# Three stretches of an elementwise product and GELU: the short stretch moved from the end of the y loads to their front

## The chip, the cores and the metric

The kernel runs on one core of one Trainium2 chip. The metric is the device time of one execution in microseconds (us), taken as the median of several runs. The profile is one further execution, recorded by the hardware profiler; its times run from the start of the first recorded instruction.

## The reference

Two float32 arrays of 1024 x 4096 are multiplied element by element, and the tanh form of GELU is applied to the product:

```
z = x * y
out = 0.5 * z * (1 + tanh(sqrt(2 / pi) * (z + 0.044715 * z ** 3)))
```

Each array has 16.78 MB. Both are read once and one is written once, 50.33 MB in all.

## The kernel before

The kernel is written without a scheduler: every queue's order and every wait is laid down by hand. The flat array is cut into three stretches, PIECES, and each stretch is spread over the 128 partitions so that a partition's share is one contiguous row in memory. The stretches are 1280, 16384 and 15104 columns of float32 for each partition, that is rows of 5 KB, 64 KB and 59 KB. They are called here the small, the first large and the second large stretch. All of x has its place in the buffer `xs`; y has a smaller buffer `ys` of 20440 columns, whose parts are used again. The product is written over x in `xs`, GELU is applied there in place, and the stores read `xs`.

- **Loads of x.** `load_x(0)` (small, issued by SP) and `load_x(1)` (first large, issued by ACT) are moved by `_hoist` to the very front of the program, ahead of its opening barriers. `load_x(2)` (second large) is issued by SP later.
- **Loads of y.** `Y_LOADS` lists start column, end column and place in `ys` of each load of y, in order of issue; all go through SP. Before the change these are the first large stretch, the second large one, and the small one last. SP waits for the small x (`sem_x[0]`) before it issues the first of them. `Y_FREE[i]` is the number of finished multiplications that load i waits for because it writes over an older part of `ys`.
- **VectorE (DVE)**, line 98, multiplies in pieces whose widths `STEPS` gives: four of 4096, then seven of 2048 and one of 768, then one of 1280. It waits for the load of y in question at line 95.
- **ScalarE (ACT)**, line 106, applies GELU to each piece after its multiplication.
- **Stores**, line 115, are issued by SP in the order of `STORES`: first large, second large, small. SP executes in order, so each store stands behind all loads and behind every earlier store's wait. The first store also waits (line 114 and the line before it) for `sem_y[-2]`, the last load of y but one, so that it is queued when one load is still in front of it.
- **End.** SP waits for all stores but the last (line 117), clears the semaphores (line 120) and then waits for the last store (line 121).

SP's DMAs all go through one queue, which the profile calls q1; ACT's single load has a queue of its own, q10.

Of the kernel before, what the change touches and what calls it, by code (L numbers as in the profile page):

```python
# [1 line left out]

# [4 lines left out]


F32 = mybir.dt.float32
GELU = mybir.ActivationFunctionType.Gelu_apprx_tanh  # L10

PIECES = [(0, 1280), (1280, 17664), (17664, 32768)]

Y_LOADS = [(1280, 17664, 4056), (17664, 32768, 0), (0, 1280, 15104)]

Y_FREE = [0, 3, 4]

STEPS = [[4096] * 4, [2048] * 7 + [768], [1280]]  # L20
STORES = [(1280, 17664), (17664, 32768), (0, 1280)]
Y_BUF = 20440


def _hoist(nc, issued):

    here = nc.cur_bb.bb.instructions
    first = nc.main_func.blocks[0].instructions
    for ins in issued:
        del here[next(k for k, i in enumerate(here) if i is ins or i.name == ins.name)]  # L30
    engine = issued[0].engine
    at = next(
        k
        for k, i in enumerate(first)
        if i.engine == engine and type(i).__name__ == "InstDrain"
    )
    first[at:at] = issued


@with_exitstack  # L40
def kernel(
    ctx: ExitStack,
    tc: tile.TileContext,
    x: bass.AP,
    y: bass.AP,
    out: bass.AP,
):
    nc = tc.nc
    P = nc.NUM_PARTITIONS

    def columns(t, a, b):

        flat = t.flatten_outer_dims().rearrange("r c -> (r c)")
        pa, pb = next(q for q in PIECES if q[0] <= a and b <= q[1])
        return flat[P * pa : P * pb].rearrange("(p c) -> p c", p=P)[:, a - pa : b - pa]


    tc.close()
    tc.compile()  # L59

    xs = nc.alloc_sbuf_tensor("xs", [P, PIECES[-1][1]], F32).ap()
    ys = nc.alloc_sbuf_tensor("ys", [P, Y_BUF], F32).ap()
    sem_x = [nc.alloc_semaphore(f"sem_x{i}") for i in range(len(PIECES))]
    sem_y = [nc.alloc_semaphore(f"sem_y{i}") for i in range(len(Y_LOADS))]
    sem_mul = nc.alloc_semaphore("sem_mul")
    sem_act = nc.alloc_semaphore("sem_act")
    sem_o = [nc.alloc_semaphore(f"sem_o{i}") for i in range(len(STORES))]

    def load_x(i, engine=nc.sync):
        a, b = PIECES[i]  # L70
        return engine.dma_start(out=xs[:, a:b], in_=columns(x, a, b)).then_inc(sem_x[i], 16)

    def load_y(i):
        a, b, r = Y_LOADS[i]
        return nc.sync.dma_start(
            out=ys[:, r : r + b - a], in_=columns(y, a, b)
        ).then_inc(sem_y[i], 16)

    _hoist(nc, [load_x(0).ins])
    _hoist(nc, [load_x(1, nc.scalar).ins])  # L80
    nc.sync.wait_ge(sem_x[0], 16)
    load_y(0)
    load_x(2)
    for i in range(1, len(Y_LOADS)):
        if Y_FREE[i]:
            nc.sync.wait_ge(sem_mul, Y_FREE[i])
        load_y(i)

    n = 0
    done = {}  # L90
    for i, (a, b, r) in enumerate(Y_LOADS):
        for j, (xa, xb) in enumerate(PIECES):
            if xa <= a < xb:
                nc.vector.wait_ge(sem_x[j], 16)
        nc.vector.wait_ge(sem_y[i], 16)  # L95
        c = a
        for w in STEPS[i]:
            nc.vector.tensor_mul(  # L98
                out=xs[:, c : c + w],
                in0=xs[:, c : c + w],  # L100
                in1=ys[:, r + c - a : r + c - a + w],
            ).then_inc(sem_mul, 1)
            n += 1
            done[c + w] = n
            nc.scalar.wait_ge(sem_mul, n)
            nc.scalar.activation(  # L106
                out=xs[:, c : c + w], in_=xs[:, c : c + w], func=GELU
            ).then_inc(sem_act, 1)
            c += w

    for i, (a, b) in enumerate(STORES):
        if i == 0:
            nc.sync.wait_ge(sem_y[-2], 16)
        nc.sync.wait_ge(sem_act, done[b])
        nc.sync.dma_start(out=columns(out, a, b), in_=xs[:, a:b]).then_inc(sem_o[i], 16)
    for i in range(len(STORES) - 1):
        nc.sync.wait_ge(sem_o[i], 16)
    nums = sorted(s.num for s in [*sem_x, *sem_y, *sem_o[:-1], sem_mul, sem_act])
    assert nums == list(range(nums[0], nums[-1] + 1))
    nc.sync.sem_clear(range(nums[0], nums[-1] + 1))  # L120
    nc.sync.wait_ge(sem_o[-1], 16).then_inc(sem_o[-1], -16)


# [1 line left out]
_INS = ['x', 'y']  # L125
_OUTS = [((1024, 4096), 'float32')]


# [23 lines left out]
```

## Time and profile before

| what | value |
|---|---|
| median of 3 runs | 119.79 us (119.72 to 119.82) |
| span of the profiled execution | 118.5 us (118.52 in the trace) |
| own time of the profiled execution | not recorded beyond its span; 119.79 - 118.52 = 1.27 us is how far the runs' median lies above it |
| VectorE busy | 35.2 us (30%), 13 instructions |
| ScalarE busy | 31.0 us (26%), 14 instructions |
| DMA | 50.33 MB, mean 425 GB/s; q1 82.2% and q10 16.5% of 16 engines' span |
| DMAs | 3 loads of x, 3 loads of y, 3 stores |

A share of "16 engines' span" is the sum of the times that all packets of a queue took, divided by 16 times the span. A packet here is one row of one partition, so each of the nine DMAs has 128 data packets, 8 for each of the 16 DMA engines, and one 4-byte packet for each engine that raises the semaphore. "us to landing" counts from a DMA's issue to its semaphore's last increment, the time spent behind other DMAs included.

### The profile page before, as it was taken

The page shows a single profiled execution, that of the slowest core. Times are in us where ns is not written, and L with a number is a line of the kernel's source. Part 1 is how long each engine was busy: PE and PEld are TensorE (multiplying, and loading weights), DVE is VectorE, ACT ScalarE, POOL GpSimd, SP SyncE. Part 2 cuts the span into 40 slices and gives each one's busy share as a digit, 9 for nine tenths or more (in the row PEclk, how much of TensorE's full clock was granted, in tenths as well). Part 3 has the DMA queues.
Part 4 walks back from the last instruction along what each step waited for, and adds up shares of the span by engine and source line. Part 5 has one row for each costly group of instructions (what it writes and reads, how often), then busy time and mean ns, then how long its engine had stood idle before and what let it go on. Part 6 is the DMA issues. An engine that isn't in the chain of part 4 may idle for free.

```text
span 118.5 us, 82 instructions
## 1 busy us (share of the span) xinstructions
DVE 35.2 (30%) x13; ACT 31.0 (26%) x14; POOL 0.2 (0%) x4
## 2 busy tenths in 40 slices
DVE  0000000000000069999920000059999940000000
ACT  4000000000000000977975000006998990000000
POOL 0000000000000000000000000000000000000000
DMA  9888899889988897797797797798899887977975
GB/s 492 382 382 382 354 575 487 354 354 398 664 354 354 354 652 326 326 652 326 326 632 347 326 632 347 326 575 354 354 531 531 354 354 326 652 326 326 652 326 221
DMA packets 1296, 50.33 MB, mean 425 GB/s; under 512 B 144, under 2 KB 144, under 8 KB 528
## 3 DMA queue, kind: packets, MB, share of 16 engines
q1 hardware_dynamic: 1152, 41.94, 82.2%
q10 hardware_dynamic: 144, 8.39, 16.5%
HBM read 33.55 MB, written 16.78 MB: 425 GB/s over the span
## 4 chain that ended last, share of the span: by engine, by line
DMA 55%; DVE 24%; ACT 3%; issue 1%; DVEq 0%
DMA ys<-in_y_dram 43%; DVE xs L98 24%; DMA xs<-in_x_dram 11%; ACT xs L106 3%; DVEq L95 0%
## 5 line engine op out<-in xcount | busy, mean ns | idle before, releaser
L98 DVE TENSOR_TENSOR xs<-xs,ys 128x2048 f32<-128x2048 f32 (+3 forms) x13 | 35.2, 2777 | 60.9 <-DMA ys<-in_y_dram 60.9
L106 ACT ACTIVATE xs<-xs 128x2048 f32<-128x2048 f32 (+3 forms) x13 | 29.7, 2301 | 65.1 <-DVE xs L98 65.1
L106 ACT ACT_TABLE_LOAD x1 | 1.3, 1283 | 1.6 <-PEq L59 1.6
L136 POOL MEMSET const-bfloat16-1.0<- 128x1 bf16 x1 | 0.1, 103 | 0.0
L136 POOL MEMSET const-uint8-127<- 128x1 uint8 x1 | 0.1, 102 | 0.0
L136 POOL MEMSET const-float32-0.0<- 128x1 f32 x1 | 0.1, 100 | 0.2 <-issue 0.2
L136 POOL MEMSET const-float32-1.0<- 128x1 f32 x1 | 0.1, 99 | 0.0
## 6 DMA issues: line engine op xcount, KB each, us to landing
xs<-in_x_dram SPq DMA_DIRECT2D x1, 7552.0 KB, 46.5
ys<-in_y_dram SPq DMA_DIRECT2D x1, 7552.0 KB, 22.5
out_dram<-xs SPq DMA_DIRECT2D x1, 7552.0 KB, 20.4
xs<-in_x_dram SPq DMA_DIRECT2D x1, 640.0 KB, 13.6
ys<-in_y_dram SPq DMA_DIRECT2D x1, 640.0 KB, 19.7
out_dram<-xs SPq DMA_DIRECT2D x1, 640.0 KB, 20.8
xs<-in_x_dram ACTq DMA_DIRECT2D x1, 30.4
ys<-in_y_dram SPq DMA_DIRECT2D x1, 29.0
```

What stands on the lines that cost most here:

```text
L98: nc.vector.tensor_mul(out=xs[:, c : c + w], in0=xs[:, c : c + w], in1=ys[:, r + c - a : r + c - a + w],).then_inc(sem_mul, 1)
L106: nc.scalar.activation(out=xs[:, c : c + w], in_=xs[:, c : c + w], func=GELU).then_inc(sem_act, 1)
L136: nc = _bacc.Bacc("TRN2", target_bir_lowering=False, num_devices=1)
```

## The change

The small stretch of y becomes the first load of y, issued without a wait for the small x. The load of y's second large stretch is cut in two, rows of 11264 columns (44 KB) and of 3840 columns (15 KB). The widths of the multiplications follow: the small piece comes first, the second large stretch is five pieces of 2048 and one of 1024 for the first part, one of 2048 and one of 1792 for the second. The small stretch is stored second, between the two large ones. `sem_y[-2]`, for which the first store waits, is now the 44 KB load.

```diff
-Y_LOADS = [(1280, 17664, 4056), (17664, 32768, 0), (0, 1280, 15104)]
+Y_LOADS = [(0, 1280, 0), (1280, 17664, 4056), (17664, 28928, 0), (28928, 32768, 11264)]
 
-Y_FREE = [0, 3, 4]
+Y_FREE = [0, 0, 3, 4]
 
-STEPS = [[4096] * 4, [2048] * 7 + [768], [1280]]
-STORES = [(1280, 17664), (17664, 32768), (0, 1280)]
+STEPS = [[1280], [4096] * 4, [2048] * 5 + [1024], [2048, 1792]]
+STORES = [(1280, 17664), (0, 1280), (17664, 32768)]
 Y_BUF = 20440
...
     _hoist(nc, [load_x(0).ins])
     _hoist(nc, [load_x(1, nc.scalar).ins])
-    nc.sync.wait_ge(sem_x[0], 16)
     load_y(0)
+    load_y(1)
     load_x(2)
-    for i in range(1, len(Y_LOADS)):
+    for i in range(2, len(Y_LOADS)):
         if Y_FREE[i]:
             nc.sync.wait_ge(sem_mul, Y_FREE[i])
         load_y(i)
```

## The prediction

> **What bounds the kernel now.** I read the page's DMA part first, because VectorE and ScalarE are busy for only 30% and 26% of the span.
>
> ```profile
> DMA packets 1296, 50.33 MB, mean 425 GB/s; under 512 B 144, under 2 KB 144, under 8 KB 528
> ...
> q1 hardware_dynamic: 1152, 41.94, 82.2%
> q10 hardware_dynamic: 144, 8.39, 16.5%
> HBM read 33.55 MB, written 16.78 MB: 425 GB/s over the span
> ```
>
> The two queues' packets together take 82.2 + 16.5 = 98.7% of the time of 16 DMA engines. Of 118.5 us an engine is without a packet for only 1.3%, 1.5 us. Next, the waits of SP's queue and the chain in order of time:
>
> ```profile
> SPq L75 <- DVE xs L98: 45.4, 2, 41.4
> SPq L117 <- DMA out_dram<-xs: 18.9, 1, 18.9
> SPq L115 <- ACT xs L106: 18.7, 2, 17.9
> SPq L115 <- DMA ys<-in_y_dram: 14.5, 1, 14.5
> SPq L75 <- DMA xs<-in_x_dram: 12.0, 1, 12.0
> ```
>
> ```profile
> 0.00 13.55 DMA xs<-in_x_dram
> 13.55 0.02 issue
> 13.57 28.99 DMA ys<-in_y_dram
> ...
> 55.78 22.47 DMA ys<-in_y_dram
> ```
>
> and last the DMA issues with their times to landing:
>
> ```profile
> xs<-in_x_dram SPq DMA_DIRECT2D x1, 7552.0 KB, 46.5
> ys<-in_y_dram SPq DMA_DIRECT2D x1, 7552.0 KB, 22.5
> out_dram<-xs SPq DMA_DIRECT2D x1, 7552.0 KB, 20.4
> xs<-in_x_dram SPq DMA_DIRECT2D x1, 640.0 KB, 13.6
> ys<-in_y_dram SPq DMA_DIRECT2D x1, 640.0 KB, 19.7
> out_dram<-xs SPq DMA_DIRECT2D x1, 640.0 KB, 20.8
> ```
>
> The waits look large, and the chain puts 13.55 us on the small load of x. But a wait of the issuing engine costs time only if the DMA engines run dry behind it. Adding issue time (from the timeline: 0, 13.57, 13.96, 55.78, 60.12, 78.27, 96.55, 97.71) and time to landing gives the landings: small x 13.55, first large x about 30.5, first large y 42.56, second large x 60.41, second large y 78.25, small y 79.82, then the stores at 99.19, 116.98 and 118.49. From 42.56 on each follows the one before by its own size: 60416-byte rows after 17.85 us (7.73 MB, 433 GB/s), 5120-byte rows after 1.57 us, 65536-byte rows after 19.37 us. These are eight packets in a row on each engine: 2.230 us, 0.196 us, 2.42 us each. A straight line through the first two has 0.0368 us for 1000 bytes and 0.0079 us for each packet whatever its size. So the kernel is a single uninterrupted stream of packets, and its time is the sum of packets plus what lies at the two ends. The packet records of the trace say the same: the first packet starts at 1.01 us, the last ends at 118.12, and between them the engines stand without a packet for about 0.09 us each at 79 us, and little else.
>
> **Where the 1.5 us of idle time lie.** 1.01 us ahead of the first packet; 118.52 - 118.12 = 0.40 us after the last one; the 0.09 us at 79 us, where the small y has run out (79.0 on the first engine) before the first store, issued at 78.27, has its packets ready (first at 79.11, so 0.84 us after the issue). The change touches only the last of these directly.
>
> **The change, part by part.**
>
> *The wait for the small x goes, and the small y is issued at about 1.5 us* (SP's last opening barrier ends then, by the trace). SP's 12.0 us of waiting vanish, but its cover was ACT's load of the first large x: from 10.8 us, when the last packet of the small x ends, to 14 us q10 alone kept all 16 engines in packets of 2.42 us. Nothing is gained. Now the small y's eight packets per engine stand there alternately with q10's. They cost the 1.57 us that they no longer cost at 78.25. The first large y therefore lands 1.57 later, at 42.56 + 1.57 = 44.1, and the second large x at 62.0. If the wait's cover were missing, it would cost up to 13.57 - 10.8 = 2.8 us.
>
> *The multiplications of the small stretch* (1.48 us on VectorE, 1.25 on ScalarE) move from 94.6 us into the empty time before 44 us, as the small y should land at around 25 us (alternating with the five large packets of x that are left at 10.8). Free.
>
> *The second large y as 44 and 15 KB rows.* The loads wait for two and three multiplications of 4096, at a pitch of 17.43 / 4 = 4.36 us: issued at about 53 and 57 us, while the second large x runs until 62.0. The cover is 5 to 9 us where it was 60.41 - 55.78 = 4.6. If it were gone, each microsecond late would cost one. Packets: by the line above 45056 bytes take 1.666 us and 15360 bytes 0.573. Eight of each are 13.33 + 4.58 = 17.91, where one load took 17.85: **+0.06 us**, and 0.01 for one more semaphore packet. The landings are 75.3 and 79.9.
>
> [...]
>
> *The first store* is issued when the 44 KB load lands, at 75.3, with 4.6 us of packets ahead instead of 1.57. The 0.84 us from issue to packet are covered now, so the 0.09 us at 79 us goes: **between -0.09 and 0**, since the engine that ends last had no such gap (its small y ends at 79.38, after 79.11). I take -0.04.
>
> *The order of the stores.* Small one second: its wait on ScalarE was met long before. The last store waits for the final GELU. VectorE starts the second large stretch at 75.4 and takes 5 x 2.2 + 1.1, ending at 87.6; the 15 KB part lands at 79.9, so VectorE goes on to 91.8 and ScalarE to about 93.5. The store is needed when the small store runs out, at 79.9 + 19.4 + 1.6 = 100.8: 7 us of cover, where the one before had 98.5 - 96.55 = 2. Nothing is gained, for it was covered already. The bytes cost the same in either order.
>
> *The end.* The last packet is now 59 KB. From the last packet's end to the last landing I count 0.44 us for that store in the trace and 0.37 for the small one: **+0.07**. Engines ended within 0.16 us of each other after either store; without the pause at 79 us to line them up they may end up to 0.38 apart (the spread at 79 us), whence a bound of +0.2. The semaphores were cleared at 117.06, under the last store, and will be cleared under it again, at about 101.
>
> Sum against the profile's 118.52: +0.07 - 0.04 + 0.07 = +0.1, so 118.6; with the 1.27 us by which the median of 119.79 lies above the span, **119.9 us**. Known bounds: -0.09 to +0.35.
>
> **Rivals.** A difference under 0.2%, 0.24 us, is about what a measurement of this kernel can tell from none.
>
> *Slower: alternating small and large packets costs more than their bytes.* In the opening 17.43 MB (both x loads and the first large y) land at 42.56. At the stream's 433 GB/s they need 40.25; with 1.01 in front and 0.36 behind that makes 41.6, so 0.95 us are lost there, in the only stretch in which small packets run beside a second queue. If they are the price of 0.64 MB of small packets among large ones, a second 0.64 MB pays it again: 119.9 + 0.95 = 120.8. It decides from 0.24 us on, when each of the 128 packets takes 30 ns more than 196. Against it: the packet records have 196 ns for most small packets between 4 and 11 us (196 to 225 by the microsecond), and 282 on average from 1 to 2 us, where they run alone. So most of the loss belongs to the start, which stays. Price by that row: up to 8 x 0.029 = 0.23.
>
> *Faster: the queue that is kept full gains.* If with q1 empty from 10.8 to 13.6 us the engines had run below their rate, the small y would fill gaps, together with the 0.09 at 79 us. The most that could come back is idle time, 1.5 - 1.01 - 0.40 = 0.1 us, and the 0.45 us by which the two x loads' packets exceed their later durations: 119.79 - 0.55 = 119.25. Against it: the slow packets lie in the first microseconds, ahead of the small y.
>
> *The engines' work becomes the bound* is excluded: they would have to end 7 us later.
>
> **How the numbers follow.** Forecast (no difference to be measured, 119.9): 0.74. Alternation, or another gap in the stream, slower by over 0.24 us: 0.17. Faster by over 0.24 us: 0.09. The forecast's own range is 119.7 to 120.15. The price of 0.23 for packets among large ones on top of it reaches 120.3, and half of what the faster case could give reaches 119.55, which leaves under 2 in 10 outside.
>
> **What would show it.** Right: landings near 25 (small y), 44.1, 62.0, 75.3, 79.9, 99.2, 100.8 and 118.6; the queues' shares adding to about 98.8%; SP's wait on the small x gone with the first large y landing later, not earlier. Wrong: shares under 98%, small-y packets over 226 ns, or a landing at which the difference to before jumps by over 0.2 us outside the places named.

## The result and the profile after

The change makes the kernel slower: 120.95 us (median of 4 runs, 120.77 to 120.99) against 119.78 us for the kernel before (4 runs beside it), a ratio of 1.009, interval 1.0077 to 1.0102. That is 1.17 us. The profiled execution is the fastest of the four, with a span of 119.4 us where the kernel before has 118.5, so its profile shows 0.9 us of the 1.17.

First the page's DMA part of the changed kernel:

```profile
DMA packets 1440, 50.33 MB, mean 421 GB/s; under 512 B 160, under 2 KB 160, under 8 KB 544
q1 hardware_dynamic: 1296, 41.94, 82.4%
q10 hardware_dynamic: 144, 8.39, 16.3%
HBM read 33.55 MB, written 16.78 MB: 421 GB/s over the span
```

The shares again add to 98.7%. No gap has opened, and yet the same bytes take 0.9 us longer: 421 GB/s instead of 425. An engine that is busy with a slow packet is busy, so the share cannot show where the time went. The times to landing can. Here are SP's issues (start, length, what) and the DMA issues with their times to landing, both of the changed kernel:

```profile
1.56 0.81 SPq L75 DMA_DIRECT2D ys<-in_y_dram  x2
53.08 4.66 SPq L75 DMA_DIRECT2D ys<-in_y_dram  x2
75.38 18.54 SPq L115 DMA_DIRECT2D out_dram<-xs  x3
```

```profile
xs<-in_x_dram SPq DMA_DIRECT2D x1, 7552.0 KB, 59.6
out_dram<-xs SPq DMA_DIRECT2D x1, 7552.0 KB, 25.8
ys<-in_y_dram SPq DMA_DIRECT2D x1, 5632.0 KB, 22.3
ys<-in_y_dram SPq DMA_DIRECT2D x1, 1920.0 KB, 23.3
```

The 44 KB rows are issued at 53.08 and land 22.3 later, at 75.4. The 15 KB rows are issued at 57.4 (the second issue ends at 53.08 + 4.66, and one takes 0.33) and land 23.3 later, at 80.7. Between the two landings lie 5.3 us, where eight packets of 0.573 us make 4.6. All the other landings, from the trace, against the forecast:

| landing | forecast | measured |
|---|---|---|
| small y | about 25 | 24.8 |
| first large y | 44.1 | 44.2 |
| second large x | 62.0 | 62.0 |
| 44 KB rows of y | 75.3 | 75.4 |
| 15 KB rows of y | 79.9 | 80.7 |
| first large store | 99.2 | 100.1 |
| small store | 100.8 | 101.6 |
| second large store | 118.6 | 119.4 |

There is one jump, in the 15 KB load, and everything behind it is late by the same 0.8 to 0.9. The packet records show its inside: the packets of that load that start before 77.2 us take 0.573 to 0.595 us, those after it up to 1.376. The mean of the 128 is 0.696, so each engine spends 8 x 0.696 = 5.57 us on them instead of 4.58: 0.99 us lost. All other packets from 6 us on have their usual length, within 0.02 us.

What happens shortly before 77.2 is the first store: it is issued at 75.38, when the 44 KB rows have landed. It has to wait until the 15 KB rows are through. In the kernel before it was issued at 78.27, as SP's line of that kernel shows:

```profile
78.27 19.77 SPq L115 DMA_DIRECT2D out_dram<-xs  x3
```

Four other things are new there too, and the first experiments tell them apart: rows of 15 KB taken out of rows of 59 KB, VectorE and ScalarE at work beside the load, a second store issued at once behind the first, and the opening.

### The profile page after: what moved, and what is told of

It is laid out like the page before. It is cut to its first block, busy times and chain, and to the rows that moved or that the text cites. A ratio compares the mean times of both kernels' runs of the same rounds, so it can differ in the third digit from the quotient of the medians.

```text
span 119.4 us, 84 instructions
## 1 busy us (share of the span) xinstructions
DVE 35.3 (30%) x13; ACT 31.1 (26%) x14; POOL 0.2 (0%) x4
## 4 chain that ended last, share of the span: by engine, by line
DMA 54%; DVE 20%; ACT 1%; issue 1%; SPq 0%; DVEq 0%
DMA ys<-in_y_dram 54%; DVE xs L98 20%; ACT xs L106 1%; SPq L75 0%; DVEq L95 0%
## 5 line engine op out<-in xcount | busy, mean ns | idle before, releaser
L98 DVE TENSOR_TENSOR xs<-xs,ys 128x2048 f32<-128x2048 f32 (+4 forms) x13 | 35.3, 2779 | 56.5 <-DMA ys<-in_y_dram 56.5
L106 ACT ACTIVATE xs<-xs 128x2048 f32<-128x2048 f32 (+4 forms) x13 | 29.8, 2302 | 60.9 <-DVE xs L98 60.8
## 6 DMA issues: line engine op xcount, KB each, us to landing
ys<-in_y_dram SPq DMA_DIRECT2D x1, 5632.0 KB, 22.3
ys<-in_y_dram SPq DMA_DIRECT2D x1, 1920.0 KB, 23.3
ys<-in_y_dram SPq DMA_DIRECT2D x1, 640.0 KB, 23.3
```

The source lines that it names most:

```text
L98: nc.vector.tensor_mul(out=xs[:, c : c + w], in0=xs[:, c : c + w], in1=ys[:, r + c - a : r + c - a + w],).then_inc(sem_mul, 1)
L106: nc.scalar.activation(out=xs[:, c : c + w], in_=xs[:, c : c + w], func=GELU).then_inc(sem_act, 1)
```

## Experiments

Each time stands beside runs of the kernel before on the same chip. "Loss" is the time by which an engine's eight packets of the last loads exceed their undisturbed length, mean over the engines, from the packet records of the run's one profiled execution.

**The opening and the order of the stores, without the cut.** The small y first, the 59 KB load whole. The store's wait for `sem_y[-2]` then falls on the first large y, so that the store is issued at 65.3 us.

```diff
-Y_LOADS = [(0, 1280, 0), (1280, 17664, 4056), (17664, 28928, 0), (28928, 32768, 11264)]
+Y_LOADS = [(0, 1280, 0), (1280, 17664, 4056), (17664, 32768, 0)]
-Y_FREE = [0, 0, 3, 4]
+Y_FREE = [0, 0, 4]
-STEPS = [[1280], [4096] * 4, [2048] * 5 + [1024], [2048, 1792]]
+STEPS = [[1280], [4096] * 4, [2048] * 7 + [768]]
```

> The small y first, without the wait for the small x, but the 59 KB load whole; the first store is then issued at about 65 us, when GELU on the first large stretch is done, with some 14 us of the second large y's load still ahead of it in SP's queue. In the changed kernel the 15 KB packets took 0.70 us on average instead of 0.57 and those started after 77.2 us, 1.9 us after the first store's issue, took up to 1.38: 0.99 us lost. Queued-store theory (loads slow down once a store's packets stand behind them on the same queue): the 60416-byte packets after about 67 us take longer than 2.23 us; if the loss lasts as long as the store stands there (some 40% over 12 us) 5 us slower than the changed kernel, about 125; if it is paid once at the transition, about 120.9 again. Partial-row theory (rows of 15 KB at a pitch of 59 KB are slow to read): no partial rows, so 2.23 us throughout and 119.9. Compute theory (VectorE and ScalarE beside the last load): the second large stretch is computed only after its load, so 119.9.

Measured: 120.92 us against 119.79, ratio 1.0099 (1.0082 to 1.0116). Without any row of 15 KB, and with the second large stretch computed after its load, the loss is there, 1.27 us. SP's issues and the load of this run:

```profile
65.29 34.16 SPq L115 DMA_DIRECT2D out_dram<-xs  x3
```

```profile
ys<-in_y_dram SPq DMA_DIRECT2D x1, 7552.0 KB, 23.6
```

The load is issued at 57.24 and lands at 80.8, 18.9 us after the second large x (61.9) instead of 17.85. Only the last of the eight packets of each engine is slow, 3.2 to 3.9 us instead of 2.23; the seven before it are normal, although the store had been queued for 11 us. So partial rows and compute are not needed for the loss, and it is bounded: it falls on the last 60 KB of each engine, however long the store has stood there.

**One store issued instead of two.** Stores in their old order.

```diff
-STORES = [(1280, 17664), (0, 1280), (17664, 32768)]
+STORES = [(1280, 17664), (17664, 32768), (0, 1280)]
```

> The changed kernel with the stores in their old order, so that one store instead of two is issued while the 15 KB load is under way. Two-stores theory (it is the second store's issue, at 75.8 us, that disturbs the load): the 15 KB packets are back at 0.573 us and the time at 119.9. Queued-store, partial-row and compute theories: they stay at 0.70 us on average, 120.9.

Measured: 120.97 us, ratio 1.0103 (1.0088 to 1.0118); 15 KB packets 0.717 us on average, loss 1.16. The second store is not the cause, nor is the order of the stores.

**VectorE held back until all of y is there.**

```diff
+        if i == 2:
+            nc.vector.wait_ge(sem_y[3], 16)
         nc.vector.wait_ge(sem_y[i], 16)
```

> The changed kernel with VectorE held back until the 15 KB load has landed too; its work then ends at about 97 us and the last store is issued at about 98.7, still ahead of the 100.8 at which it is needed. Compute theory: 15 KB packets at 0.573 us, 119.9. Queued-store, two-stores and partial-row theories: 0.70 us on average, 120.9.

Measured: 120.88 us, ratio 1.0098 (1.0079 to 1.0116); 15 KB packets 0.698 us. With both engines idle during the load the loss is the same.

**The cut alone**, in the kernel before; the store is issued when the 15 KB rows have landed, with the small y still ahead of it.

```diff
-Y_LOADS = [(1280, 17664, 4056), (17664, 32768, 0), (0, 1280, 15104)]
+Y_LOADS = [(1280, 17664, 4056), (17664, 28928, 0), (28928, 32768, 11264), (0, 1280, 15104)]
-Y_FREE = [0, 3, 4]
+Y_FREE = [0, 3, 3, 4]
-STEPS = [[4096] * 4, [2048] * 7 + [768], [1280]]
+STEPS = [[4096] * 4, [2048] * 5 + [1024], [2048, 1792], [1280]]
```

> The kernel before with its 59 KB load of y cut into 44 and 15 KB and nothing else; the small y stays last, and the first store is issued when the 15 KB rows have landed, at about 78.3 us. Partial-row theory: 15 KB packets at 0.70 us, total about 120.8. Queued-store theory: 0.573 us, as no store stands behind them, and about 119.85. Compute theory: VectorE starts on the 44 KB part at about 73.7 us, ScalarE at 76, beside the 15 KB load, so packets slowed after 76 and up to 120.8.

Measured: 119.88 us, ratio 1.0007 (0.9998 to 1.0016); every 15 KB packet 0.573 to 0.578 us. Partial rows and one DMA more cost 0.09 us here, and by the interval no more than 0.2.

**Less load ahead of the store.** The second large y cut into 13824 and 1280 columns, then into 12544 and 2560; the rest as in the changed kernel. The first of the two:

```diff
-Y_LOADS = [(0, 1280, 0), (1280, 17664, 4056), (17664, 28928, 0), (28928, 32768, 11264)]
+Y_LOADS = [(0, 1280, 0), (1280, 17664, 4056), (17664, 31488, 0), (31488, 32768, 13824)]
-Y_FREE = [0, 0, 3, 4]
+Y_FREE = [0, 0, 4, 4]
-STEPS = [[1280], [4096] * 4, [2048] * 5 + [1024], [2048, 1792]]
+STEPS = [[1280], [4096] * 4, [2048] * 6 + [1536], [1280]]
```

> The changed kernel with the second large y cut into 13824 and 1280 columns, so that the first store is issued with 8 x 5 KB packets (1.57 us) ahead of it, as in the kernel before; opening and order of the stores are the changed kernel's. So far a whole 59 KB load with the store queued 14 us ahead lost 1.27 us, all of it in the last packet of each engine, and the 15 KB load lost 1.0 us in the last four packets. Queued-store theory (a load's last 60 KB per engine are slowed if the store's packets stand ready behind them): the store's packets are ready only some 0.85 us after its issue, so at most the last 0.7 us is slowed; 5 KB packets near 0.20 us, total 119.8 to 120.0. Rival, that the opening or the new order of the stores carries the loss: 120.9.

Measured: 119.91 us against 119.86, ratio 1.0005 (0.9995 to 1.0015). Opening and store order are those of the changed kernel and cost nothing that can be measured. The idle gap at 79 us is back with the short cover: 0.2 us for each engine.

> The same with 12544 and 2560 columns: 8 x 10 KB packets, by the line through the sizes 0.385 us each, 3.1 us ahead of the store. Queued-store theory: the store stands ready for the last 2.2 us, about the last 60 KB of each engine, so most of the loss: 0.7 to 1.1 us, total 120.5 to 120.9. If the loss grows evenly with the time that the store waits, 1.0 x 2.2 / 3.7 = 0.6 us, total 120.4.

Measured: 120.02 us against 119.86, ratio 1.0018 (1.0007 to 1.0029); 10 KB packets 0.387 us, no loss and no gap, though the median lies 0.16 us above that of the kernel before. My expectation of 0.7 to 1.1 us missed. Either smaller packets are spared, or the store, issued at 77.05, came too late to do harm.

**The store only after all loads.**

```diff
-            nc.sync.wait_ge(sem_y[-2], 16)
+            nc.sync.wait_ge(sem_y[-1], 16)
```

> The changed kernel, its first store issued only when the 15 KB load has landed. Queued-store theory: all 15 KB packets at 0.573 us; but the engines stand idle from the load's end to the store's first packet, 0.36 us of landing and 0.85 us from issue to packet, 1.2 us: total 119.85 + 1.2 = 121.05. Partial-row theory: 0.70 us on average and the idle time as well, 122.0.

Measured: 121.47 us, ratio 1.0137 (1.0122 to 1.0152). All 15 KB packets are at 0.576 us again, but each engine stands idle for 1.6 us on average, from its own last packet to the store's first at 80.70, 0.84 us after the issue at 79.86. I had counted 1.2, from the last engine's end.

**A small store first**, so that 5 KB packets instead of 64 KB ones stand behind the loads.

```diff
-STORES = [(1280, 17664), (0, 1280), (17664, 32768)]
+STORES = [(0, 1280), (1280, 17664), (17664, 32768)]
```

> The changed kernel with the small store first, so that packets of 5 KB instead of 64 KB stand behind the 15 KB load. If the loss comes from the size of the packet that stands behind the loads (the engine working ahead on a 64 KB packet), the 15 KB packets lose much less, 0.1 to 0.4 us, and the total is about 120.1 to 120.3; if any store there does it, 1.0 us is lost as before, 120.9.

Measured: 120.79 us, ratio 1.0079 (1.0064 to 1.0094); 15 KB packets 0.690 us. Whether the store's packets have 5 KB or 64 KB makes next to no difference.

**Packet size or time of issue: 10 KB rows with an early store.** The kernel of 12544 and 2560 columns without the first store's wait, so that it is issued at 65.3.

```diff
-        if i == 0:
-            nc.sync.wait_ge(sem_y[-2], 16)
```

> The kernel with 12544 and 2560 columns, whose 10 KB packets were not slowed (0.387 us each, store issued at 77.05 us, 2.0 to 2.6 us before the load's packets end), but with its first store issued at about 65.4 us, as soon as GELU on the first large stretch is done. Time-since-issue theory (a queued store slows the last 60 KB per engine of the loads ahead of it only once some 1.9 to 2.4 us have passed since its issue): the 10 KB packets are slowed now, about 1.0 to 1.3 us lost, total 120.9 to 121.2. Packet-size theory (packets of 10 KB or less are not slowed): 0.387 us and 120.0.

Measured: 120.92 us against 119.76, ratio 1.0094 (1.0076 to 1.0112); 10 KB packets 0.523 us on average, loss 1.1. Small packets are not spared.

**The changed kernel with only the store's issue moved**, to the end of the first multiplication on the 44 KB rows, 77.77 us.

```diff
-            nc.sync.wait_ge(sem_y[-2], 16)
+            nc.sync.wait_ge(sem_mul, 6)
```

> The changed kernel (15 KB rows last), its first store issued not at the landing of the 44 KB rows, 75.4 us, but after the first multiplication on them, at about 77.7; its packets should be ready at about 78.6, the load's packets end at 79.0 to 79.4. Time-since-issue theory: 15 KB packets at 0.573 us, no idle time, total 119.9. Packet-size theory: the last one or two packets of each engine are still slowed, total 120.2 to 120.7.

Measured: 119.90 us against 119.76, ratio 1.0009 (1.0000 to 1.0019). One wait, 2.4 us of delay, and what was 1.17 us above the kernel before is 0.14 above it: 1.03 us are back. SP's issue and the load:

```profile
77.77 16.14 SPq L115 DMA_DIRECT2D out_dram<-xs  x3
```

```profile
ys<-in_y_dram SPq DMA_DIRECT2D x1, 5632.0 KB, 22.3
ys<-in_y_dram SPq DMA_DIRECT2D x1, 1920.0 KB, 22.6
```

The 15 KB rows land after 22.6 us instead of 23.3, 4.6 us after the 44 KB rows. Their packets take 0.579 us, and no engine pauses before the store.

**The kernel before with only the store's issue moved**, the other way: the two lines that were left out for the 10 KB rows with an early store are left out of it, and the store is issued at 63.6.

> The kernel before without any part of the change, except that its first store does not wait for the second large y and is issued at about 63.8 us. Time-since-issue theory: 1.0 to 1.3 us lost in the last 60 KB of each engine's loads (the 5 KB packets and part of the last 59 KB packet), total 120.8 to 121.1. Packet-size theory: 5 KB packets at 0.196 us, and the 0.09 us of idle time at 79 us gone: 119.7. Either way it tells whether the loss belongs to the time of the store's issue alone, with opening, split and store order as before.

Measured: 121.05 us, ratio 1.0104 (1.0087 to 1.0121). SP's issues and the two last loads of y:

```profile
55.63 4.66 SPq L75 DMA_DIRECT2D ys<-in_y_dram  x2
63.62 34.44 SPq L113 DMA_DIRECT2D out_dram<-xs  x3
```

```profile
ys<-in_y_dram SPq DMA_DIRECT2D x1, 7552.0 KB, 22.6
ys<-in_y_dram SPq DMA_DIRECT2D x1, 640.0 KB, 21.0
```

The small y is issued at 59.97 and lands at 81.0, 2.7 us after the large one (55.63 + 22.6 = 78.2) where it took 1.57; its packets take 0.333 us instead of 0.196, a loss of 1.1, and the 59 KB packets ahead of them lose another 0.2. With opening, cut and order untouched, the early store alone makes the old kernel as slow as the new one.

**The store on the other queue.** Issued by ScalarE at 75.30 on q10; SP leaves it out, and with it the wait for `sem_y[-2]`.

```diff
+        if i == 2:
+            nc.scalar.wait_ge(sem_y[2], 16)
+            nc.scalar.wait_ge(sem_act, 5)
+            sa, sb = STORES[0]
+            nc.scalar.dma_start(out=columns(out, sa, sb), in_=xs[:, sa:sb]).then_inc(sem_o[0], 16)
...
-            nc.sync.wait_ge(sem_y[-2], 16)
+            continue
```

> The changed kernel with the first store issued at about 75.4 us on ScalarE's queue, q10, instead of behind the 15 KB load on q1. The engines then alternate between the queues, so the eight 15 KB packets of an engine are spread over most of the store's 19.4 us, the 15 KB load lands only near 98 us, and the work that depends on it ends at about 104, some 3 to 4 us after the engines have run out: total 123 to 125. What it is for is the length of the load's packets. If a load packet that runs beside store packets is slowed by reading and writing at once: over 0.65 us on most of the eight. If the slowing belongs to a store that stands behind loads in the same queue: 0.573.

Measured: 120.86 us, ratio 1.0095 (1.008 to 1.011), far from the 123 to 125 that I expected. The load and ScalarE's store did not alternate: the store's first packet starts at 80.08, when all 15 KB packets have started, and those are slowed just the same (0.713 us, loss 1.1). But another store was there as well. The issues of SP and of ScalarE in this run:

```profile
57.69 36.15 SPq L120 DMA_DIRECT2D out_dram<-xs  x2
75.30 0.35 ACTq L100 DMA_DIRECT2D out_dram<-xs  x1
```

As SP no longer waits for the 44 KB rows, it issues the small store at 57.69, directly behind the 15 KB load on q1; its packets start at 80.03. A small store in that place is enough for the loss, as the run with the small store first has shown. So this run does not tell whether a store on another queue slows the loads, and no other run here does.

**How the loss grows with the lead.** The store waits for a first multiplication of 1024 columns, then of 512 (`[512] + [2048] * 5 + [512]`).

```diff
-STEPS = [[1280], [4096] * 4, [2048] * 5 + [1024], [2048, 1792]]
+STEPS = [[1280], [4096] * 4, [1024] + [2048] * 5, [2048, 1792]]
...
-            nc.sync.wait_ge(sem_y[-2], 16)
+            nc.sync.wait_ge(sem_mul, 6)
```

> The changed kernel with its first store issued after a first multiplication of 1024 columns on the 44 KB rows, at about 76.6 us, 2.4 to 2.9 us before the 15 KB load's packets would end undisturbed (79.0 to 79.5). Step theory: the store's packets, ready at about 77.5, are too late for the moment at which the loss sets in in the other runs, 77.3, so no slowed packets and 119.9, or on some engines only. Growing-loss theory: none at 2.3 us, all at 3.8, so about a quarter, 0.25 to 0.4 us, total 120.2.

> The same with a first piece of 512 columns, the store issued at about 76.1 us, 2.9 to 3.4 us before the end; its packets are ready at about 77.0. Step theory: they are there before 77.3, so the whole loss, 1.0 us and 120.9. Growing-loss theory: a half to two thirds, total 120.4 to 120.6.

Measured: 120.19 and 120.41 us against 119.93, ratios 1.0018 (1.0007 to 1.0029) and 1.0049 (1.0033 to 1.0066). It grows; there is no step. The second loses 0.44 us on average, but unevenly: its engines finish the load between 79.02 and 79.96, and the last one sets the end. SP's issues of the stores in these two runs and in three earlier ones (10 KB rows last, 5 KB rows last, store after all loads):

```profile
76.15 17.81 SPq L115 DMA_DIRECT2D out_dram<-xs  x3
76.63 17.21 SPq L115 DMA_DIRECT2D out_dram<-xs  x3
77.05 18.73 SPq L115 DMA_DIRECT2D out_dram<-xs  x3
78.41 18.21 SPq L115 DMA_DIRECT2D out_dram<-xs  x3
79.86 13.94 SPq L115 DMA_DIRECT2D out_dram<-xs  x3
```

The runs in order of the store's issue, the load's packets being due to end at 79.0 to 79.7 us. The cut alone and the store on the other queue are left out: the first has the store issued as in the kernel before, the second has two stores in question.

| first store issued at | kernel | loss | median, us |
|---|---|---|---|
| 63.6 | kernel before, store early | 1.3, both loads | 121.05 |
| 65.3 | whole 59 KB load | 1.27 | 120.92 |
| 65.3 | 10 KB rows last | 1.1 | 120.92 |
| 75.18 | stores in their old order | 1.16 | 120.97 |
| 75.27 | VectorE held back | 1.00 | 120.88 |
| 75.38 | changed kernel | 0.99 | 120.95 |
| 75.38 | small store first | 0.93 | 120.79 |
| 76.15 | first piece 512 | 0.44 | 120.41 |
| 76.63 | first piece 1024 | 0.13 | 120.19 |
| 77.05 | 10 KB rows last | 0.02 | 120.02 |
| 77.77 | first piece 2048 | 0.05 | 119.90 |
| 78.41 | 5 KB rows last | 0.01 and 0.2 idle | 119.91 |
| 79.86 | after all loads | 0.03 and 1.6 idle | 121.47 |

In these runs it takes a store behind a load. In the changed kernel the 44 KB packets, with the 15 KB load queued behind them from 57.4 on, stay at 1.667 us, and the first store's packets, with the small store queued behind them from 75.8 on, at 2.418.

No order here beats the kernel before.

## Why the prediction was wrong

It forecast no measurable difference, 119.9 us, and 119.55 to 120.3 as the range. Point by point:

- **What bounds the kernel**: right, one uninterrupted stream of packets. The step from there to the sum was too quick. I took a packet's length as fixed by its size, since all later packets of the kernel before had theirs, and so looked only for gaps. The kernel before could not show otherwise, for its only load packets ahead of a waiting store are the last 0.3 us of the small y.
- **The opening**: right. The landings at 24.8, 44.2 and 62.0 are those of the forecast, and the run with 5 KB rows last (119.91 against 119.86) shows that it costs nothing that can be measured. SP's 12 us wait was covered, and the multiplications moved for free.
- **The cut**: right; 0.573 and 1.667 us per packet were worked out as 0.573 and 1.666, and the cut alone gives 119.88. The Trainium skill's "DMA: Bandwidth & Descriptors" (Anatomy of one DMA) puts about 2.0 us of fixed cost on a DMA that GpSimd issues. None here is: SP issues this load, and with the cut one DMA more costs 0.09 us.
- **The first store, issued with 4.6 us of packets ahead instead of 1.57**: this step failed. I wrote "between -0.09 and 0" and took -0.04, counting the longer cover as a gain. The gap of 0.09 us did go. But the store's presence lengthened the packets ahead of it by 0.99 us for each engine. Moving this one issue gives 1.03 of the 1.17 us back, and in the kernel before it costs 1.29. The wait for `sem_y[-2]` was the same line of code with another meaning: the load behind which the store is let in now had 4.6 us still to follow it instead of 1.57.
- **The order of the stores**: right. They cost no more in the new order, and waited for nothing. They even take 0.17 us less (19.34 + 1.57 + 17.83 us per engine against 19.43 + 17.88 + 1.60). That goes with the pause, not with the order: the first store's large packets take 2.418 or 2.419 us on average in every run without a pause ahead of it, and 2.43 in the four runs with one.
- **The end**: two terms were mis-sized. Engines out of step were allowed 0.38 us; without the pause at 79 us they end within 0.58 us of each other, where the kernel before has 0.16. And from the last packet's end to the last landing it took 0.35 us, not 0.44, so the +0.07 did not come. Closing the gap at 79 us gains nothing, as the run with the issue at 77.77 shows: no gap, hardly a loss, and still 119.90. Why is not shown. In its profile the engines end 0.54 us apart, and the 44 KB packets, long before the store, take 1.682 us instead of 1.666, 0.13 us for each engine.
- **The rivals**: the slower one named another mechanism and is refuted, though its 120.8 lies close. The small y's packets among the large ones took 0.196 us each. The faster one had no gaps to fill, as said. Of the signs that I named for being wrong, the last one, a landing that jumps by over 0.2 us elsewhere, is what led to the cause.

Two rules of the Trainium skill's page "DMA: Bandwidth & Descriptors" look different after these runs. Its "Rules for kernel authors" advise, to overlap a DMA with compute, to issue it early so that its fixed cost overlaps; for a store behind loads the early issue cost 0.9 to 1.3 us here, and an issue about 1.5 us before the loads' end cost the loads nothing to speak of (0.05 us). Its "Queues, rings and completion order" says that an engine takes turns between queues with work, packet by packet; in the opening the small and the first large x do so, but the store that ScalarE issued at 75.30 had no packet recorded before 80.08, behind all packets of the load. From then on it took turns with the small store on SP's queue. Here the measurement decides.

What stays open is what the engines do in those last 2 us. In the runs that lose 0.1 us or more with a store from 75.2 us on, the first packets slowed by over 0.1 us start 1.3 to 1.9 us after its issue; where it has stood for 11 us or more, the loss still falls only on about the last 2 us (60 KB per engine) of the loads. Its size hardly depends on the packets' sizes (5 to 59 KB in the load, 5 or 64 KB in the store); whether it depends on the queue is open. That would fit engines that take up the store ahead of time while still loading, but no record shows it.

## What to carry to other kernels

In a stream bound by DMA, the moment at which a store is let in behind loads is a parameter of its own. Too late leaves the engines idle, too early slows the loads ahead of it, and here the loads lost nothing to speak of, and no engine paused, with an issue 1.3 to 2.6 us before their end. Even so, the two kernels with such an issue (77.77 and 77.05) ran 0.14 and 0.16 us longer than the kernel before. When a change moves what a wait refers to, cost the new moment, not only the cover. A busy share that stays the same does not show that nothing slowed down: compare landings pair by pair, and look where a difference jumps.

## What was not expected of the hardware

A store queued early slows the loads ahead of it, by 0.9 to 1.3 us in all and only over about their last 60 KB per engine. In the runs without a pause before the stores the engines end the 59 KB store 0.4 to 1.0 us apart; in the four runs with one, of 0.1 us and more, they end it within 0.2 us.
